# A down projection in Strassen products: its right operands made at the end of the gate and up stage instead of in the projection itself

## The chip, the cores and the metric

The kernel runs on one core of a Trainium2 chip. The metric is the time of one execution on the device, in microseconds (us). Five engines work side by side, each with its own queue of instructions that it takes in order: TensorE (PE, the matmuls), VectorE (DVE), ScalarE (ACT), GpSimd (POOL) and SyncE (SP, which here does nothing but issue DMAs). They wait for one another by semaphores. Matmuls read SBUF and write PSUM banks; a DMA moves between SBUF and DRAM.

## The reference

One layer of a decoder for 1024 tokens of width 1024. Only the last part matters here, the feed-forward network and what follows it:

```python
def _swiglu(h, w_gate, w_up, w_down):
    return (jax.nn.silu(h @ w_gate) * (h @ w_up)) @ w_down
...
        h = _rmsnorm(x, g_ffn[layer]) * (1.0 + sc2) + sh2
        x = x + gt2 * _swiglu(h, w_gate[layer], w_up[layer], w_down[layer])
    return _rmsnorm(x, g_final)
```

The hidden width is 2816, that is 22 blocks of 128. All is float32.

## The kernel before

A float32 product is formed from three matmuls in a shorter format: each operand is split into a high and a low part (`split`: ScalarE casts the high part, another engine, mostly VectorE, subtracts it from the operand to get the low part), and high by high, high by low and low by high are summed in PSUM. On top of this, large products are done by Strassen's scheme in Winograd's form: two by two blocks need 7 products instead of 8, for which sums of blocks are made ahead. Class `Strassen` holds one such group. Its left operands come from weights: `load` fetches a raw tile `Wraw` by SyncE's queue (two buffers), `left` makes the sums `Wsum` on GpSimd (four buffers) and splits each operand into a `Wop` tile (six buffers). `product` runs 3 matmuls for each of the `nk` blocks of the inner dimension, 128x512 each. The right operands, 7 of them in split form, come from a class `Rights`, which makes them of four blocks; they lie in SBUF tiles called `cell`. Results gather in three PSUM banks (a, b, c) of a group; bank a is added to by products 0, 5, 6 and 3 in turn, and what it holds after each is needed, so that it is read between them.

The feed-forward part has three stages.

Gate and up: the 22 blocks of the hidden width are taken two by two. Each of 11 `Pair` objects has one group for gate and one for up, with nk = 4: 14 products of 12 matmuls, 168 in all. `keep` copies bank a to an `x` tile on ScalarE; `g_done` and `u_done` form silu(gate) times up, four tiles of 128x512 for each pair. `st` stores each of these by SyncE to a DRAM tensor `actd`.

Down: the first 20 blocks of the hidden width are taken in 5 chunks of 4. In each chunk there are four groups `Down` with nk = 2 (42 matmuls each), two by two (`dd` = 0 and 1), in which the same right operands are used. 20 groups make 840 matmuls. The right operands of a chunk are made by `dsplit`: it loads the four `actd` blocks back, makes the sums on VectorE (`sub`, line 277), and splits 14 tiles of 128x512 (lines 83 and 84, cell<-cell). This is done one chunk ahead, while the products of `dd` = 1 run. The results are scaled and added to the residual `x1`: of the seven values of a group four are added by VectorE (line 1226) and three are kept by ScalarE (line 1220) and added by GpSimd (line 1228).

Tail: the last two blocks of the hidden width are multiplied without Strassen, and the final norm and the output follow.

The order of the instructions on each engine is set by a scheduler that goes by the order of the code, with a bonus of priority where the code stands under `tc.high_priority`.

## Time and profile before

| | us |
|---|---|
| median of 3 runs | 1693.13 |
| lowest and highest of them | 1692.99, 1709.35 |
| profiled execution | 1701.24 |
| its span, first to last instruction | 1699.5 |
| TensorE busy in the span | 1554.4 (91%) |
| VectorE busy | 1208.4 (71%) |
| ScalarE busy | 864.6 (51%) |
| GpSimd busy | 669.0 (39%) |

The first row is what a changed kernel is compared with. The durations of single instructions come from the profiled execution, whose own time is 8 us above the median. Busy shares are means over stages with different limits, so the stages are read apart: gate and up ends and Down begins near 1420 us after the span's start, the tail begins at 1655 us.

### The profile page before, as it was taken

The page shows a single profiled execution, that of the slowest core. Times are in us where ns is not written, and L with a number is a line of the kernel's source. Part 1 is how long each engine was busy: PE and PEld are TensorE (multiplying, and loading weights), DVE is VectorE, ACT ScalarE, POOL GpSimd, SP SyncE. Part 2 cuts the span into 40 slices and gives each one's busy share as a digit, 9 for nine tenths or more (in the row PEclk, how much of TensorE's full clock was granted, in tenths as well). Part 3 has the DMA queues.
Part 4 walks back from the last instruction along what each step waited for, and adds up shares of the span by engine and source line. Part 5 has one row for each costly group of instructions (what it writes and reads, how often), then busy time and mean ns, then how long its engine had stood idle before and what let it go on. Part 6 is the DMA issues. An engine that isn't in the chain of part 4 may idle for free.

```text
span 1699.5 us, 21993 instructions
## 1 busy us (share of the span) xinstructions
PE 1554.4 (91%) x7306; PEld 1274.6 (75%) x7306; DVE 1208.4 (71%) x2373; ACT 864.6 (51%) x1691; POOL 669.0 (39%) x575
## 2 busy tenths in 40 slices
...
GB/s 328 187 117 306 162 199 241 142 209 207 293 215 179 208 185 214 168 174 138 83 351 143 149 75 93 136 81 100 93 87 93 109 127 241 75 86 88 74 50 99
DMA packets 156065, 267.88 MB, mean 158 GB/s; under 512 B 34844, under 2 KB 70348, under 8 KB 150704
## 3 DMA queue, kind: packets, MB, share of 16 engines
q1 hardware_dynamic: 107952, 224.45, 39.7%
...
## 4 chain that ended last, share of the span: by engine, by line
PE 46%; DVE 11%; DMA 3%; issue 2%; ACT 2%; POOL 1%; DVEq 0%; ACTq 0%; POOLq 0%; SPq 0%
PE bk L219 27%; PE acc L891 3%; PE S L782 3%; DVE Wop L84 3%; PE bk L87 3%; PE bk L88 3%; PE bk L89 3%; DVE cell L84 3%; PE pv L823 2%; PE tr L804 2%; DVE x L1226 2%; DMA vbd<-ev 2%; DVE cell L277 1%; DMA Wraw<-wdown 1%; DVE P L784 0%
## 5 line engine op out<-in xcount | busy, mean ns | idle before, releaser
L219 PE MATMUL bk<-cell,Wop 128*128 128x512 f32 x4056 | 967.3, 399 | 59.3 <-DVE Wop L84 25.2
L219 PEld LDWEIGHTS bk<-cell,Wop 128*128 128x128 f32 x4056 | 769.1, 191 | 251.4 <-DVE Wop L84 40.2
L189 POOL TENSOR_TENSOR Wsum<-Wraw 128x512 f32<-128x512 f32 (+1 forms) x120 | 171.8, 1433 | 533.0 <-DVE Wop L84 310.9
L83 ACT CAST Wop<-Wsum 128x512 fp32r<-128x512 f32 (+1 forms) x241 | 131.5, 548 | 231.2 <-PE bk L219 132.3
L84 DVE TENSOR_TENSOR Wop<-Wsum,Wop 128x512 fp32r<-128x512 f32 (+1 forms) x241 | 182.7, 765 | 90.9 <-ACT Wop L83 89.6
L84 DVE TENSOR_TENSOR Wop<-Wraw,Wop 128x512 fp32r<-128x512 f32 (+2 forms) x182 | 147.6, 818 | 59.6 <-ACT Wop L83 54.4
L83 ACT CAST Wop<-Wraw 128x512 fp32r<-128x512 f32 (+2 forms) x182 | 104.9, 591 | 146.7 <-PE bk L219 60.3
L782 PE MATMUL S<-cell,cell 128*128 128x128 f32 (+8 forms) x480 | 119.1, 363 | 11.8 <-DMA cell<-ksd 7.9
L789 ACT ACTIVATE P<-P,mx 128x512 f32<-128x512 f32 (+7 forms) x128 | 99.3, 778 | 30.7 <-DVE mx L784 18.2
L84 DVE TENSOR_TENSOR pl<-tr,ph 128x512 fp32r<-128x512 f32 (+1 forms) x160 | 98.3, 630 | 22.2 <-ACT ph L83 21.1
L891 PE MATMUL acc<-cell,w 128*128 128x512 f32 x408 | 113.8, 407 | 0.1
L1228 POOL TENSOR_TENSOR x<-x 128x512 f32<-128x512 f32 x60 | 96.2, 1609 | 35.8 <-DVE x L1226 24.8
L162 ACT COPY x<-bk 128x512 f32<-128x512 f32 x92 | 53.4, 586 | 104.2 <-PE bk L219 102.2
L804 PE MATMUL tr<-ident,P 128*128 128x128 f32 x576 | 93.5, 280 | 5.8 <-ACT P L792 4.7
L782 PEld LDWEIGHTS S<-cell,cell 96*128 96x128 f32 (+1 forms) x480 | 80.6, 196 | 21.1 <-DMA cell<-ksd 8.3
L87 PE MATMUL bk<-cell,Wop 128*128 128x512 f32 (+1 forms) x240 | 91.9, 383 | 2.9 <-ACT Wop L83 1.9
L823 PE MATMUL pv<-ph,v 128*128 128x256 f32 (+1 forms) x320 | 88.3, 293 | 6.8 <-ACT ph L83 6.0
L83 ACT CAST ph<-tr 128x512 fp32r<-128x512 f32 (+1 forms) x160 | 83.2, 544 | 15.9 <-PE tr L804 12.7
L88 PE MATMUL bk<-cell,Wop 128*128 128x512 f32 (+1 forms) x240 | 91.0, 380 | 0.0
L89 PE MATMUL bk<-cell,Wop 128*128 128x512 f32 (+1 forms) x240 | 89.8, 377 | 0.0
L891 PEld LDWEIGHTS acc<-cell,w 128*128 128x128 f32 x408 | 77.2, 195 | 13.5 <-DVE ev L922 0.3
L823 PE MATMUL pv<-pl,v 128*128 128x256 f32 x320 | 82.3, 292 | 4.8 <-DVE pl L84 4.5
...
## 6 DMA issues: line engine op xcount, KB each, us to landing
...
```

The costliest lines, as they stand in the source:

```text
L83: ACT.copy(hi, src)
L84: eng.tensor_sub(lo, src, f32(hi))
L87: PE.matmul(ps, w[0], a[0], start=first, stop=False)
L88: PE.matmul(ps, w[0], a[1], start=False, stop=False)
L89: PE.matmul(ps, w[1], a[0], start=False, stop=last)
L189: POOL.tensor_tensor(t, a, b, op=op)
L219: PE.matmul(ps, w[:, wi, k], t[k][:, ti], start=start and k == 0 and n == 0, stop=k == self.nk - 1 and n == 2, skip_group_check=True)
L782: anchor[0] = PE.matmul(s, q[:, i * P:i * P + P], k[:, c * wd:c * wd + wd], start=pi == 0, stop=pi == len(passes) - 1)
L789: ACT.activation(t[:, :n], t[:, :n], AF.Exp, bias=mx[:, 0:1], scale=-1.0, accum_out=mx[:, 1:2])
L804: anchor[0] = PE.transpose(tr[:, co:co + P], self.p[a][:, kb * P:kb * P + P], ident)
L823: anchor[0] = PE.matmul(pv[:, o if l else 0:], v[:, kk], p[:, l:r], start=kk == 0 and n == 0, stop=last and l > 0 and n == 1, skip_group_c ...
L891: PE.matmul(ps, w[wi][:, k0 + k], act(k, ai, hf), start=k == 0 and n == 0, stop=k == nk - 1 and n == 2)
```

## The change

The right operands of Down are no longer made in Down. `u_done` of pairs 0 to 9 splits the operand that a finished tile is by itself (indices 0, 1, 2), and with the pair's last tile makes the four that are sums or differences (four subtractions on VectorE) and splits these. One pair gives one of the two inner blocks of a chunk. Each of the 14 parts is stored by a DMA that ScalarE issues, into the DRAM tensors `tod` (256 KB each). Pairs 0 to 2, whose first tile is made long before the others, store it in `actd` and load it again. Pair 10, which the tail uses, stores as before.

Down then loads the operands in split form, product by product (`load_op`, two loads of 512 KB), one chunk ahead, by SyncE. The products of a group run in another order (`OD`), and all seven values are added to `x1` by VectorE (`into`), with the bonus of priority; nothing is kept by ScalarE or added by GpSimd. The rows of `w_down` are laid out in another order ahead of the launch, to go with the blocks of a pair. A tile `al`, which holds nothing and lies ahead of the cells, grows from 32 to 96 bytes per partition, so that the cells' addresses move by 64 bytes.

```diff
@@ -146,6 +146,7 @@
     actd = [dp.tile([P, T], F32, name=f"actd{f}") for f in range(FFB)]
+    tod = [[dp.tile([P, 2, H], F32, name=f"tod{pr}_{i}") for i in range(7)] for pr in range(FFB // 2 - 1)]
 
@@ -295,7 +296,7 @@
 
-    pool(ctx, "al", side="right").tile([P, 8], F32, name="al")
+    pool(ctx, "al", side="right").tile([P, 24], F32, name="al")
     bq = pool(ctx, "bq", side="right")
@@ -1118,7 +1119,7 @@
         def __init__(self, pr, load=True):
-            self.pr, self.silu = pr, {}
+            self.pr, self.silu, self.early = pr, {}, not load
             self.g = Strassen(wgate[pr], 4, R2.ops, keep, self.g_done, load)
@@ -1138,7 +1139,28 @@
                 DVE.tensor_mul(t, t, s)
-            st(actd[2 * self.pr + pos[0]][:, hsl[pos[1]]], t)
+            f, hf = 2 * self.pr + pos[0], pos[1]
+            if self.pr == FFB // 2 - 1 or pos == (0, 0) and self.early:
+                st(actd[f][:, hsl[hf]], t)
+            elif pos != (0, 1):
+                self.put({(0, 0): 0, (1, 0): 1, (1, 1): 2}[pos], t)
+            else:
+                b0, b1, b2, b3 = [self.silu[p] for p in ((0, 0), (0, 1), (1, 0), (1, 1))]
+                if self.early:
+                    b0 = X()
+                    ld(b0, actd[2 * self.pr][:, hsl[0]])
+                    self.put(0, b0)
+                for o, x_, y in ((b0, b1, b0), (b1, b3, b1), (b3, b3, b0), (b2, b2, b3)):
+                    DVE.tensor_sub(o, x_, y)
+                for i, b in ((5, b3), (4, b0), (6, b1), (3, b2)):
+                    self.put(i, b, True)
+
+        def put(self, i, b, inplace=False):
+            hi = X(F32R)
+            lo = b.bitcast(F32R) if inplace else X(F32R)
+            split(b, hi, lo)
+            for l, t in enumerate((hi, lo)):
+                ACT.dma_start(out=tod[self.pr][i][:, l], in_=f32(t))
 
@@ -1161,6 +1183,7 @@
     p0 = Pair(0)
+    p0.early = True
     p0.steps(OR[:1])
@@ -1188,61 +1211,66 @@
 
-    tcell = cycle([*range(4), *range(8, 26)])
-    rcell = cycle([4, 5, 6, 7, 26, 27])
-    TT = lambda *_: cell(next(tcell))
-
-    def load_act(f):
-        t = cell(next(rcell), dt=F32)
-        t = [t[:, 0], t[:, 1]]
-        ld2(t, actd[f])
-        return t
-
-    def dsplit(f0, nk):
-        R = Rights([load_act(f0 + j) for j in range(2 * nk)], nk, TT, lambda j: DVE)
-        R.early()
-        R.late()
-        return R.ops
-
-    ops = dsplit(0, 2)
-    x1 = [X2() for _ in range(8)]
-    for j in range(8):
-        ld2(x1[j], x1d[j])
+    tcell = cycle(range(28))
+    OD = (0, 1, 5, 4, 6, 2, 3)
+
+    def load_op(ops, ci, i):
+        ops[i] = [cell(next(tcell)) for _ in range(2)]
+        for k in range(2):
+            ld(f32(ops[i][k]), tod[2 * ci + k][i])
+
+    ops = [None] * 7
+    x1 = [None] * 8
+    for n, i in enumerate(OD):
+        load_op(ops, 0, i)
+        if n in (1, 3):
+            for j in ((0, 2), (1, 3))[n // 2]:
+                x1[j] = X2()
+                ld2(x1[j], x1d[j])
 
     class Down(Strassen):
+
+
         def __init__(self, ci, dp_, ops):
             self.dp = dp_
-            super().__init__(wdown[ci * 4 + dp_], 2, ops, self.keep_d, self.done_d)
-
-        def keep_d(self, ps, pos):
-            j = 2 * self.dp + pos[0]
-            t = X()
-            ACT.activation(t, ps, AF.Copy, scale=modc[:, 40 + j:41 + j])
-            return t
-
-        def done_d(self, pos, ps, s):
+            super().__init__(wdown[ci * 4 + dp_], 2, ops, None, None)
+
+        def into(self, name, pos):
             j = 2 * self.dp + pos[0]
             xs = x1[j][pos[1]]
-            DVE.scalar_tensor_tensor(xs, ps, modc[:, 40 + j:41 + j], xs, op0=OP.mult, op1=OP.add)
-            if s is not None:
-                POOL.tensor_add(xs, xs, s)
+            DVE.scalar_tensor_tensor(xs, self.bk[name], modc[:, 40 + j:41 + j], xs, op0=OP.mult, op1=OP.add)
+
+        def step(self, i):
+            name, start, pos = {0: ("a", True, (0, 0)), 1: ("b", True, (0, 0)), 5: ("a", False, (0, 1)),
+                                4: ("c", True, (1, 1)), 6: ("a", False, (1, 1)), 2: ("c", False, (0, 1)),
+                                3: ("a", False, (1, 0))}[i]
+            self.product(i, name, start)
+            with tc.high_priority(offset=HP):
+                self.into(name, pos)
 
...
             prs = [Down(ci, 2 * dd + e, ops) for e in range(2)]
-            if dd == 1:
-                if ci < NC - 1:
-                    nxt = dsplit(4 * ci + 4, 2)
-                else:
-                    tail = []
-                    for f in (20, 21):
-                        raw = load_act(f)
-                        tl = [TT(), TT()]
-                        for hf in range(2):
-                            split(raw[hf], tl[hf][:, 0], tl[hf][:, 1])
-                        tail.append(tl)
-            for i in OR:
+            if ci == 0 and dd == 0:
+                for j in range(4, 8):
+                    x1[j] = X2()
+                    ld2(x1[j], x1d[j])
+            if dd == 0:
+                nxt = [None] * 7
+            if dd == 1 and ci == NC - 1:
+                tail = []
+                for f in (20, 21):
+                    raw = cell(next(tcell), dt=F32)
+                    raw = [raw[:, 0], raw[:, 1]]
+                    ld2(raw, actd[f])
+                    tl = [cell(next(tcell)) for _ in range(2)]
+                    for hf in range(2):
+                        split(raw[hf], tl[hf][:, 0], tl[hf][:, 1])
+                    tail.append(tl)
+            for n, i in enumerate(OD):
+                if ci < NC - 1 and (7 * dd + n) % 2 == 0:
+                    load_op(nxt, ci + 1, OD[(7 * dd + n) // 2])
                 for q in prs:
@@ -1390,7 +1418,8 @@
         "wup": _quarters(g["w_up"][0]),
-        "wdown": np.concatenate([_quarters(g["w_down"][0][i * 512:i * 512 + 512]) for i in range(5)], axis=0),
+        "wdown": np.concatenate([_quarters(g["w_down"][0][i * 512:i * 512 + 512].reshape(2, 2, P, D).transpose(1, 0, 2, 3).reshape(512, D))
+                                 for i in range(5)], axis=0),
         "wdl": _blocks(g["w_down"][0][2560:]).transpose(1, 0, 2).reshape(P, 16, P),
...
```

How the order of instructions moves is shown at three places. First ScalarE between two pairs of gate and up. Before:

```order
L1131 ACTIVATE x<-x 128x512 [waits DVE_49]
L83 CAST Wop<-Wsum 128x512 [waits PE_49,Pool_49]
L162 COPY x<-bk 128x512 [waits PE_49]
L83 CAST Wop<-Wsum 128x512 [waits Activation_49]
L162 COPY x<-bk 128x512 [waits DMAHW6_49,PE_49]
L83 CAST Wop<-Wsum 128x512 [waits Activation_49]
L83 CAST Wop<-Wsum 128x512 [waits PE_49,Pool_49]
```

After, at the same place (COPY is `keep`, `tod` a store, CAST x<-x the split of an operand):

```order
L83 CAST x<-x 128x512 [waits DVE_49]
L83 CAST x<-x 128x512 x2
L83 CAST x<-x 128x512 [waits DVE_49]
L1163 DMA tod_5_200<-x 128x512 [waits DMAHW0_49,Activation_49]
L1163 DMA tod_4_199<-x 128x512 [waits DMAHW2_49,Activation_49]
L1163 DMA tod_5_200<-x 128x512 [waits DMAHW3_49,DVE_49]
L1163 DMA tod_4_199<-x 128x512 [waits DMAHW4_49,DVE_49]
L1163 DMA tod_6_201<-x 128x512 [waits DMAHW5_49,Activation_49]
L1163 DMA tod_6_201<-x 128x512 [waits DMAHW6_49,DVE_49]
L1163 DMA tod_3_198<-x 128x512 [waits DMAHW7_49,Activation_49]
L1163 DMA tod_3_198<-x 128x512 [waits DMAHW0_49,DVE_49]
L163 COPY x<-bk 128x512 x2
```

Behind the last silu product of a pair stand now four casts and eight stores, four of which wait for VectorE; the two copies of the next pair's bank a come after them. Up to the gate and up stage, the rows of all engines are as before, and TensorE's matmuls follow in the same order.

Second, VectorE in a chunk of Down while `dd` = 1 runs. Before:

```order
L1226 SCALAR_TENSOR_TENSOR x<-bk,modc,x 128x512 [waits PE_49]
L84 TENSOR_TENSOR Wop<-Wsum,Wop 128x256 [waits Activation_49]
L84 TENSOR_TENSOR Wop<-Wsum,Wop 128x256 [waits PE_49,Activation_49]
L84 TENSOR_TENSOR cell_13956<-cell_13914,cell_13956 128x512 [waits Activation_49]
L84 TENSOR_TENSOR cell_13957<-cell_13917,cell_13957 128x512 [waits Activation_49]
L1226 SCALAR_TENSOR_TENSOR x<-bk,modc,x 128x512 [waits PE_49]
L84 TENSOR_TENSOR Wop<-Wsum,Wop 128x256 [waits Activation_49] x2
L1226 SCALAR_TENSOR_TENSOR x<-bk,modc,x 128x512 [waits PE_49]
L84 TENSOR_TENSOR cell_13962<-cell_13914,cell_13962 128x512 [waits Activation_49]
L84 TENSOR_TENSOR cell_13963<-cell_13917,cell_13963 128x512 [waits Activation_49]
L84 TENSOR_TENSOR Wop<-Wsum,Wop 128x256 [waits Activation_49]
L1226 SCALAR_TENSOR_TENSOR x<-bk,modc,x 128x512 [waits PE_49]
```

After:

```order
L1241 SCALAR_TENSOR_TENSOR x<-bk,modc,x 128x512 [waits DVE_49,PE_49]
L84 TENSOR_TENSOR Wop<-Wraw,Wop 128x256 [waits DMAHW4_49,Activation_49]
L84 TENSOR_TENSOR Wop<-Wraw,Wop 128x256 [waits Activation_49]
L1241 SCALAR_TENSOR_TENSOR x<-bk,modc,x 128x512 [waits PE_49]
L84 TENSOR_TENSOR Wop<-Wraw,Wop 128x256 [waits Activation_49]
L1241 SCALAR_TENSOR_TENSOR x<-bk,modc,x 128x512 [waits PE_49]
L84 TENSOR_TENSOR Wop<-Wsum,Wop 128x256 [waits Activation_49]
L1241 SCALAR_TENSOR_TENSOR x<-bk,modc,x 128x512 [waits PE_49]
L84 TENSOR_TENSOR Wop<-Wsum,Wop 128x256 [waits Activation_49]
L1241 SCALAR_TENSOR_TENSOR x<-bk,modc,x 128x512 [waits PE_49]
```

The subtractions that make cells are gone, and in their place stand more additions to x1: nearly every split of a `Wop` is now followed by one.

Third, SyncE at the first change of `dd` in Down. Before:

```order
L181 DMA Wraw<-wdown 128x1024 [waits DMAHW7_49,DVE_49,Pool_49]
L181 DMA Wraw<-wdown 128x1024 [waits DMAHW0_49,DVE_49,Pool_49]
L158 DMA cell_13920<-actd_162 128x512 [waits DMAHW1_49,DVE_49]
L158 DMA cell_13920<-actd_162 128x512 [waits DMAHW2_49]
L158 DMA cell_13923<-actd_163 128x512 [waits DMAHW3_49,DVE_49]
L158 DMA cell_13923<-actd_163 128x512 [waits DMAHW4_49]
L181 DMA Wraw<-wdown 128x1024 [waits DMAHW5_49,DMAHW7_49,DVE_49,Pool_49]
L181 DMA Wraw<-wdown 128x1024 [waits DMAHW0_49,DMAHW6_49,DVE_49,Pool_49]
```

After:

```order
L182 DMA Wraw<-wdown 128x1024 [waits DMAHW1_49,DVE_49,Pool_49]
L182 DMA Wraw<-wdown 128x1024 [waits DMAHW2_49,DVE_49,Pool_49]
L1220 DMA cell_14103<-tod_0_202 128x1024 [waits DMAHW3_49,PE_49]
L1220 DMA cell_14104<-tod_0_209 128x1024 [waits DMAHW4_49,PE_49]
L1220 DMA cell_14151<-tod_1_203 128x1024 [waits DMAHW5_49,PE_49]
L1220 DMA cell_14152<-tod_1_210 128x1024 [waits DMAHW6_49,PE_49]
L1220 DMA cell_14205<-tod_5_207 128x1024 [waits DMAHW7_49,PE_49]
L1220 DMA cell_14206<-tod_5_214 128x1024 [waits DMAHW0_49,PE_49]
L1220 DMA cell_14257<-tod_4_206 128x1024 [waits DMAHW1_49,PE_49]
L1220 DMA cell_14258<-tod_4_213 128x1024 [waits DMAHW2_49,PE_49]
L182 DMA Wraw<-wdown 128x1024 [waits DMAHW3_49,DVE_49,Pool_49]
```

Between two fetches of weights (in each case for two groups) stand now eight loads of 512 KB, and in the next gap six, in place of four of 256 KB; they wait for TensorE, which used the cells before, and not for VectorE.

## Rows read from the trace of the kernel before

**Rows 1.** Busy time in 50 us stretches of gate and up; columns in the first line.

```profile
core 0: us, PE busy (x) PEld busy (x) DVE busy (x) ACT busy (x) POOL busy (x), PEclk, DMA share, GB/s
1050.00:1100.00 50.00, 50.00 (x221) 41.04 (x220) 28.72 (x36) 16.14 (x27) 21.84 (x16) 1.00 0.37 132
...
1350.00:1400.00 50.00, 50.00 (x220) 41.07 (x219) 26.43 (x44) 21.55 (x38) 13.13 (x10) 1.00 0.39 132
```

**Rows 2.** The same in 25 us stretches of Down, columns as in rows 1.

```profile
1400.00:1425.00 25.00, 25.00 (x111) 20.49 (x110) 22.70 (x44) 13.04 (x28) 17.86 (x7) 1.00 0.71 230
...
1500.00:1525.00 25.00, 19.92 (x81) 14.28 (x80) 24.97 (x33) 13.03 (x30) 14.87 (x12) 1.00 0.27 84
...
1600.00:1625.00 25.00, 23.97 (x103) 18.86 (x102) 23.66 (x35) 13.97 (x32) 18.39 (x16) 1.00 0.12 43
1625.00:1650.00 25.00, 25.00 (x111) 20.53 (x110) 21.09 (x31) 12.16 (x29) 20.40 (x20) 1.00 0.25 78
```

**Rows 3.** Groups by line and form, 1420 to 1656 us (Down).

```profile
L219 PE MATMUL bk<-cell,Wop 128*128 128x512 f32 x828 | 205.7, 405 | 29.8 <-DVE Wop L84 21.0 <-ACT Wop L83 5.8 <-ACT cell L83 1.5
...
L1228 POOL TENSOR_TENSOR x<-x 128x512 f32<-128x512 f32 x60 | 96.2, 1609 | 35.8 <-DVE x L1226 24.8 <-ACT x L1220 8.3 <-DMA x<-x1d 1.6
L1226 DVE SCALAR_TENSOR_TENSOR x<-bk,modc,x 128x512 f32<-128x512 f32 x78 | 57.3, 739 | 3.5 <-PE bk L219 3.1 <-DMA x<-x1d 0.3
L84 DVE TENSOR_TENSOR cell<-cell,cell 128x512 fp32r<-128x512 f32 x56 | 54.0, 982 | 3.4 <-ACT cell L83 3.4
L84 DVE TENSOR_TENSOR Wop<-Wsum,Wop 128x256 fp32r<-128x256 f32 x79 | 52.4, 677 | 1.0 <-ACT Wop L83 1.0
L1220 ACT ACTIVATE x<-bk,modc 128x512 f32<-128x512 f32 x60 | 41.0, 685 | 15.1 <-PE bk L219 14.9
L84 DVE TENSOR_TENSOR Wop<-Wraw,Wop 128x256 fp32r<-128x256 f32 x56 | 39.7, 727 | 4.7 <-ACT Wop L83 4.7
...
L277 DVE TENSOR_TENSOR cell<-cell 128x512 f32<-128x512 f32 x16 | 15.8, 986 | 0.1
L277 DVE TENSOR_TENSOR cell<-cell,cell 128x512 f32<-128x512 f32 x16 | 15.5, 976 | 0.0
```

**Rows 4.** What TensorE waited for, 1420 to 1656 us: total, times, longest.

```profile
PE bk L219 <- DVE Wop L84: 21.0, 23, 2.8
```

**Rows 5.** The last chunk of Down, columns as in rows 1.

```profile
1614.00:1655.00 41.00, 39.97 (x174) 32.19 (x173) 34.61 (x49) 19.28 (x42) 32.57 (x30) 1.00 0.16 52
```

**Rows 6.** Stretches of 5 us in the last chunk, columns as in rows 1.

```profile
1610.00:1615.00 5.00, 5.00 (x23) 4.12 (x23) 3.93 (x7) 2.91 (x7) 3.32 (x3) 1.00 0.45 170
...
1630.00:1635.00 5.00, 5.00 (x24) 4.09 (x23) 2.12 (x5) 2.62 (x7) 3.20 (x5) 1.00 0.50 184
```

**Rows 7.** VectorE in order of time, in the last chunk: start, us.

```profile
1627.02 0.96 DVE L84 TENSOR_TENSOR Wop<-Wraw,Wop 128x256 fp32r<-128x256 f32 x1
...
1630.88 0.41 DVE L84 TENSOR_TENSOR Wop<-Wsum,Wop 128x256 fp32r<-128x256 f32 x1
```

**Rows 8.** Groups by line and form, 1050 to 1400 us (gate and up).

```profile
L84 DVE TENSOR_TENSOR Wop<-Wsum,Wop 128x512 fp32r<-128x512 f32 x75 | 64.4, 859 | 48.4 <-ACT Wop L83 48.0
...
L83 ACT CAST Wop<-Wsum 128x512 fp32r<-128x512 f32 x75 | 46.6, 622 | 78.9 <-PE bk L219 69.2 <-POOL Wsum L189 9.6
...
L162 ACT COPY x<-bk 128x512 f32<-128x512 f32 x50 | 29.3, 586 | 77.1 <-PE bk L219 77.1
...
L1139 DVE TENSOR_TENSOR x<-bk,x 128x512 f32<-128x512 f32 x28 | 19.3, 690 | 25.1 <-PE bk L219 16.3 <-ACT x L162 8.8
```

**Rows 9.** SyncE in order of time, end of gate and up: start, us.

```profile
1423.12 0.32 SPq L1141 DMA_DIRECT2D actd<-x  x1
```

**Rows 10.** The page: DMA bandwidth by slice, and the queue of SyncE's DMAs.

```profile
GB/s 328 187 117 306 162 199 241 142 209 207 293 215 179 208 185 214 168 174 138 83 351 143 149 75 93 136 81 100 93 87 93 109 127 241 75 86 88 74 50 99
...
q1 hardware_dynamic: 107952, 224.45, 39.7%
```

## The prediction

> **What bounds the kernel now.** I read the busy time by stretches first, because the change touches only the feed-forward part. In gate and up TensorE is busy for the whole of each of the seven stretches of 50 us from 1050 to 1400, of which the first and the last are shown, at a granted clock of 1.00 (the higher of its two levels, 2.4 GHz); VectorE has some 22 to 29 us of work in 50 there, ScalarE 16 to 22 [rows 1]. One matmul of 128x512 costs 50.00 / 220 = 0.2273 us there, and a pair of 168 takes 38.2 us. Nothing can make this stage shorter while the matmuls stay, and they stay.
>
> Down is different. In the seven stretches from 1425 to 1600, of which the one at 1500 is shown, TensorE is busy for some 20 to 22 us in 25, and VectorE for 21 to 25; in the last two stretches, where no operands for another chunk are being made, TensorE is at 23.97 and 25.00 again [rows 2]. The waits agree: of 29.8 us that TensorE stands idle from 1420 to 1656, 21.0 end with VectorE's split of a weight tile [rows 3, 4]. So VectorE bounds Down in four chunks of five. What can be won there: the stretch holds 205.7 + 29.8 = 235.5 us of busy and idle TensorE [rows 3], and 20 groups of 42 make 840 matmuls (828 have records), which at 0.2273 us are 190.9 us. The difference, **44.6 us**, is idle time and the longer matmuls about the gaps. No more than that can come back.
>
> **VectorE in Down, removed and added.** Per chunk it now has 16 additions to x1 at 0.74 us = 11.8, 28 splits of weights at about 0.70 (0.677 and 0.727) = 19.6, and for the operands 14 subtractions at 0.98 = 13.7 and 8 at 0.98 = 7.8 [rows 3]: together 52.9 us against 28 products of 6 matmuls, 28 x 1.364 = 38.2 us. Records of neighbours overlap by some 0.07 us, so that the real load is about 50. After the change the 21.5 us for operands are gone, and 12 more additions to x1 (7 in a group instead of 4) come, 8.9 us: 52.9 - 21.5 + 8.9 = 40.3 us, were the rest as slow as before. It isn't. A split of a weight takes 0.96 us beside a busy GpSimd, and 0.41 us a moment later without it [rows 7]. GpSimd loses its 12 additions of 1.609 us per chunk [rows 3], 19.3 us of the 32.6 that it is busy in the last chunk [rows 5]; 16 sums for weights are left. In the last chunk, which had 16 additions, 28 splits and 4 subtractions for the tail, VectorE was busy 34.6 us beside 32.6 us of GpSimd [rows 5]; with the short durations this would be 16 x 0.67 + 28 x 0.34 + 4 x 0.6, about 22.6 us (starts lie 0.07 closer than durations), so 12.0 us were lost beside GpSimd, 0.37 us for each of its busy microseconds. With 12 to 16 us of GpSimd left, the estimate is 28 x 0.67 + 28 x 0.34 + 0.37 x 14 = 33.5 us, between 28.3 (no loss) and 42.3 (each microsecond of GpSimd is one lost). The middle value rests on the row that is nearest to the new state, the last chunk. **TensorE becomes the bound of Down.** The Trainium skill, SBUF — State Buffer, section Who interferes with whom, says that a VectorE instruction with two inputs in SBUF and a GpSimd instruction that reads SBUF lock each other out, while one with a single SBUF input, as an addition from a PSUM bank has, isn't touched; by it the additions to x1 stay at their 0.74 us, and only the splits can lose, at worst up to the 42.3. The trace agrees that the splits are what varies [rows 7], and its 0.37 says that most of GpSimd's time meets no split.
>
> What stays lost in Down: in the last chunk TensorE was idle for about 1.0 us of 41 [rows 5], though both its refills of weights fell there, at 1610 and 1630, with TensorE at 5.00 of 5 [rows 6]. I take 1 to 2 us for each chunk, 7 in all. At the start of Down the operands of the first chunk are loaded while the last pair runs, but the x1 tiles are queued on SyncE behind stores of this pair: 0 to 4 us, I take 1.
>
> ScalarE in Down loses 14 casts and 12 copies of a bank (0.685 us each) per chunk [rows 3]; it was at half load [rows 2], so this is worth nothing by itself. That a bank is read by VectorE instead costs nothing as long as it is read within the three products (4.1 us) that lie between two products in the same bank; the bonus of priority sees to that.
>
> **Gate and up, added.** Per pair: on ScalarE seven casts at 0.622 = 4.4 us [rows 8], and 14 issues of DMAs; no row has ScalarE issue one, the nearest is SyncE's 0.32 us [rows 9], so 4.5 us, with 0 and three times that as bounds. That raises ScalarE from about 14 to some 23 us in 38.2. On VectorE 11 subtractions at 0.69 to 0.86 [rows 8], 7.6 to 9.5 us, on top of about 19. Neither gets full, and TensorE's work per pair stays 38.2 us. What counts is the order: ScalarE takes its queue in turn, and the last eight stores of a pair stand ahead of the copies of the next pair's bank a. Let T be the end of the old pair's matmuls. The block of casts and stores can start at about T + 5.5, since the cast ahead of it needs a `Wop` tile of the new pair's second product. Four casts, 2.5 us, and eight issues, 2.6 us, end at about T + 11, and VectorE's last split, behind four others of up to 0.86, no later than that. The two copies (0.586 us each [rows 8]) end at T + 12; product 5 of the new pair, which writes bank a again, is after six products of 2.73 us, at T + 16.4. So there are about 4 us of slack, and the next casts of weights have more. I take 0 to 4 us per pair as the bounds and 2 us in all ten pairs together as the value, nearest to the full stretches of rows 1. The stores take 3.7 MB per pair while the DMA engines are busy for 0.37 to 0.39 of the time or less [rows 1]. The Trainium skill, DMA: Bandwidth & Descriptors, section Issuing engines are not separate DMA queues, says that issuing from a second engine saves only the sequencer's issue time; SyncE has that to spare here, so by it the choice of ScalarE buys nothing, and its price is the 4.5 us per pair on ScalarE that the sum has.
>
> The stages ahead of gate and up keep their order; the cells' addresses move by 64 bytes. I put that at 0.
>
> **The sum.** 44.6 - 7 - 1 - 2 = 34.6 us, say 34. The profiled execution, 1701.24 us, would become 1667. It lies 8 us above the median, 1693.13, so the forecast for the median is **1659 us**.
>
> **Rivals.** (1) *Loads bound Down.* Each chunk that loads for the next moves 14 x 0.524 MB of operands and 4 x 0.524 MB of weights, 9.4 MB in 38.2 us, or 247 GB/s, where Down has about 84 now [rows 2]. For it: the fullest stretch near there moved 230 GB/s [rows 2], at which a chunk takes 41 us, and the refills of weights stand behind eight operand loads on SyncE's queue. Against it: the highest slice of the run is 351 GB/s, and SyncE's DMAs moved 224.45 MB in 39.7% of 1699.5 us of the engines, 333 GB/s while at work [rows 10]. At 230 four chunks lose 2.8 us each, and late weights after each refill perhaps 1 us more; the gain falls to about 18, 1675. At 190 GB/s it would be gone. (2) *VectorE stays the bound*: 40.3 us per chunk instead of 38.2 costs 5 x 2.1 = 10.5 us, 1670. With 42.3 it would be 5 x 4.1 = 20.5 us, 1680. (3) *The stores hold up ScalarE*, and the time gets longer: a store that waits for VectorE's low part, or for an earlier DMA, keeps the copies and the casts of weights behind it. From T + 15.2 on for the end of the block each microsecond is one of TensorE's, in each of ten pairs; at T + 19.5, nearly twice the block's length of 5.5, that is 4.3 x 10 = 43 us, more than Down gives back: 1702. Against it: over half of ScalarE's time is free [rows 1]. (4) *The cells' addresses matter* to the matmuls or the DMAs of the attention stages: no row speaks for it, and none shows cells at another address, so I can only bound it by a hundredth of the some 1000 us ahead of gate and up, 10 us either way, 1649 or 1669.
>
> **How the numbers follow.** The forecast has a chance of 0.60, rival 1 0.14, rival 2 0.10, rival 3 0.10, rival 4 0.06. One per cent, 17 us, is about what a measurement tells from no change. Faster by more than that, under 1676: 0.60, 0.08 of rival 1, 0.08 of 2 and 0.05 of 4, or 0.81. Slower, over 1710: 0.04 of rival 3. The rest, 0.15, within 1%. The range goes from 1649, where all of the 44.6 us come back, to 1687, between rivals 1 and 2 at their worse values and rival 3.
>
> **What would show it.** Right: in Down TensorE at 25 us in 25 for most stretches, VectorE under 23, the splits of weights near 0.5 us, GpSimd at a third; gate and up still at 50.00 in 50. Wrong: gaps in gate and up about 16 us after a pair's start that end with ScalarE's copy (rival 3); waits in Down that end with a DMA into `cell` or `Wraw` (1) or with VectorE's split or its addition to x1 (2); changed times ahead of 1000 us (4). The forecast would also be wrong where Down's gaps come from something that VectorE only happened to hide.

## The result, and the profile after

| | before | after |
|---|---|---|
| median, us | 1694.72 (4 runs) | 1677.15 (4 runs) |
| lowest and highest | 1692.99, 1709.35 | 1672.93, 1686.43 |
| profiled execution | 1701.24 | 1676.03 |
| its span | 1699.5 | 1674.2 |

The ratio is 0.9884, with a 95% interval from 0.9847 to 0.9922: 13 to 26 us faster, some 18 to 20 us where 34 were forecast. The profiled spans differ by more, 25.3 us, since the execution profiled of before was 6.5 us above its median and the one of after 1.1 us below.

To see where the time went I cut both traces at the starts of the activation with which ScalarE takes silu from a bank (line 1128, after 1129; one such activation in each of pairs 0, 1 and 3 to 10), at the first addition to x1, and at the first matmul of the tail. All in us:

| stretch | before | after | change |
|---|---|---|---|
| start of the span to pair 0's silu | 1046.4 | 1043.6 | -2.8 |
| pair 0's silu to pair 3's | 93.4 | 103.0 | +9.6 |
| pair 3's to pair 10's | 269.9 | 267.4 | -2.5 |
| pair 10's to the first addition to x1 | 13.6 | 18.8 | +5.2 |
| first addition to the tail's first matmul | 231.9 | 196.3 | -35.6 |
| the tail | 44.4 | 45.0 | +0.6 |

These points lie on ScalarE and VectorE, and the change moves them against TensorE's work: the first addition stands behind the second product of Down before, behind the first after, and in the change it waits for x1 while 36 of Down's 840 matmuls run ahead of it (28 before); pair 0's silu starts 3.9 us later, measured from TensorE's matmuls, than before. The expectations below count by these points. The bottleneck itself is read by counting TensorE's matmuls of the Strassen products. Each trace has all 4056 of them; the last 840 are Down's, and the mark of a pair is set 36 matmuls before its end, where its silu starts when ScalarE is in time. Full pace is the count times the steady time from one matmul's start to the next, 0.2289 us before and 0.2267 after (e1 and e2 tell why):

| stretch, by count of matmuls | before | at its full pace | after | at its full pace | change |
|---|---|---|---|---|---|
| pair 0's mark to pair 3's, 408 | 93.4 | 93.4 | 104.6 | 92.5 | +11.2 |
| pair 3's to pair 10's, 1176 | 269.2 | 269.2 | 269.7 | 266.6 | +0.5 |
| pair 10's to Down's first matmul, 36 | 8.2 | 8.2 | 8.2 | 8.2 | 0.0 |
| first chunk of Down, 168 | 48.1 | 38.5 | 49.7 | 38.1 | +1.6 |
| other four chunks, to the tail's first matmul, 672 | 190.0 | 153.8 | 157.5 | 152.3 | -32.5 |

So the four chunks of Down behind the first gave 32.5 us, the first chunk gave nothing, and 11.7 us were lost in gate and up. With the tail's 0.6 us the kernel is 18.6 us shorter from pair 0's mark on, as the medians have it. The other 6.7 us of the 25.3 lie ahead of this mark (1046.2 us before, 1039.5 after) and can't be told from scatter: in the profiled executions of the kernels below the mark lies between 1036.7 and 1049.6 us.

Busy time by stretches of the kernel after, with the columns of rows 1: two of gate and up, three of Down, three of 5 us about the passage between them, and Down from the first addition to x1 on.

```profile
1050.00:1100.00 50.00, 41.88 (x171) 33.52 (x169) 32.05 (x46) 19.57 (x35) 15.91 (x12) 0.93 0.63 228
...
1150.00:1200.00 50.00, 50.00 (x222) 41.42 (x221) 40.93 (x56) 23.29 (x41) 15.84 (x10) 1.00 0.41 151
...
1475.00:1500.00 25.00, 25.00 (x112) 20.71 (x111) 21.82 (x41) 7.30 (x19) 9.10 (x12) 1.00 0.51 183
1500.00:1525.00 25.00, 24.70 (x109) 19.88 (x108) 20.32 (x36) 6.42 (x17) 6.06 (x8) 1.00 0.76 279
...
1575.00:1600.00 25.00, 25.00 (x112) 20.44 (x110) 21.67 (x41) 9.22 (x23) 8.28 (x11) 1.00 0.19 65
...
1395.00:1400.00 5.00, 2.21 (x10) 1.50 (x8) 1.40 (x4) 0.56 (x2) 0.00 (x0) 1.00 1.05 414
...
1430.00:1435.00 5.00, 1.68 (x5) 1.16 (x4) 4.03 (x9) 0.40 (x1) 0.00 (x0) 0.81 1.05 400
...
1445.00:1450.00 5.00, 1.12 (x5) 0.58 (x4) 1.30 (x2) 0.16 (x1) 0.12 (x1) 1.00 0.88 345
...
1432.80:1629.10 196.30, 187.30 (x804) 152.24 (x804) 158.00 (x274) 52.91 (x134) 54.89 (x72) 0.98 0.54 200
```

In the middle of gate and up TensorE is full, and in Down it works 24.1 to 25 of 25 us in the stretches from 1475 to 1625, of which three are shown (where [rows 2] go down to 19.92), with VectorE at 18.6 to 22.3. But from 1050 to 1100, in pairs 1 and 2, TensorE works only 41.88 of 50 us, and at 1395, 1430 and 1445 it stands. At 1395 and 1430 the DMA share is at 1.0, with 400 GB/s and above.

Groups of instructions of the kernel after in Down (1433 to 1629 us), to set against [rows 3]:

```profile
L220 PE MATMUL bk<-cell,Wop 128*128 128x512 f32 x804 | 187.3, 395 | 9.8 <-ACT Wop L83 6.4 <-DVE x L1241 3.3
...
L1241 DVE SCALAR_TENSOR_TENSOR x<-bk,modc,x 128x512 f32<-128x512 f32 x140 | 103.5, 744 | 20.1 <-PE bk L220 18.8 <-DMA x<-x1d 0.6
L84 DVE TENSOR_TENSOR Wop<-Wsum,Wop 128x256 fp32r<-128x256 f32 x72 | 32.4, 458 | 0.0
L84 DVE TENSOR_TENSOR Wop<-Wraw,Wop 128x256 fp32r<-128x256 f32 x56 | 31.7, 582 | 15.5 <-ACT Wop L83 15.5
...
L190 POOL TENSOR_TENSOR Wsum<-Wraw 128x256 f32<-128x256 f32 x36 | 26.6, 738 | 125.6 <-DMA Wraw<-wdown 91.8 <-DVE Wop L84 33.7
```

The 140 additions to x1 take 0.744 us in the mean, as before (0.739); the splits of weights fell from 677 and 727 ns to 458 and 582, since GpSimd has little left to do. TensorE's idle time is 9.8 us in place of 29.8, and most of it ends with ScalarE's cast of a fresh weight, none with VectorE's split. TensorE in order of time, at the stands of over 2 us behind pair 0's mark (start and length of what follows a stand; the stand and what ended it in brackets):

```profile
1061.55 28.84 PE L220 MATMUL bk<-cell,Wop 128*128 128x512 f32 x120 [2.85 <-ACT x L163]
1095.65 4.36 PE L220 MATMUL bk<-cell,Wop 128*128 128x512 f32 x12 [5.27 <-DVE x L233]
...
1400.07 30.21 PE L220 MATMUL bk<-cell,Wop 128*128 128x512 f32 x132 [2.86 <-ACT x L163]
1433.61 12.51 PE L220 MATMUL bk<-cell,Wop 128*128 128x512 f32 x48 [3.32 <-DVE x L1241]
1450.30 9.99 PE L220 MATMUL bk<-cell,Wop 128*128 128x512 f32 x36 [4.18 <-ACT Wop L83]
```

Line 163 is the copy of bank a, which stands on ScalarE behind the stores of pair 0 and of pair 9; line 233 adds the base, a result of the early pass of pair 2 that is stored and loaded again, and its load came late; line 1241 is the addition to x1, which waited for x1; line 83 is the cast of a weight tile whose refill came late. After four of the five stands, all but the one that ends at 1400, the granted clock is at 0.50 (the lower of its two levels, 1.2 GHz) for 3.4 us, so that a stand costs more than its own length: the two in Down last 7.5 us, and the first chunk is 11.6 us over its full pace.

The chain of waits of the kernel after, at pair 1's last stores and about the end of the last pair (start, length):

```profile
1089.65 8.13 DMA tod<-x
...
1414.73 10.38 DMA actd<-x
...
1425.13 7.65 DMA x<-x1d
...
1441.50 8.24 DMA Wraw<-wdown
```

The chain goes through DMAs: a store of operands, `actd`, `x1`, then the refill of weights. ScalarE in order of time at the same two places (`ACTq` is its queue issuing; what ended the idle time stands in brackets):

```profile
1089.04 8.64 ACTq L1163 DMA_DIRECT2D tod<-x  x6
1097.78 1.14 ACT L83 CAST Wop<-Wsum 128x512 fp32r<-128x512 f32 x2 [8.47 <-DMA tod<-x]
...
1389.02 10.38 ACTq L1163 DMA_DIRECT2D tod<-x  x6
1399.44 1.08 ACT L163 COPY x<-bk 128x512 f32<-128x512 f32 x2 [10.36 <-DMA tod<-x]
```

ScalarE issues six stores in 8.64 us and another six in 10.38 us, where one takes 0.33 us by itself; in between it waits for earlier DMAs to land, and the casts and copies behind it wait with it. By the rows above only the second of these two stands holds TensorE (1400.07); at the first one TensorE waits for the base, and the copy for which it waited before, at 1061.55, stood behind the stores of pair 0.

The DMAs of the kernel after from 1380 to 1440 us (rate by slice of 1.5 us; count, size, median time to landing):

```profile
GB/s 348 1 0 93 322 336 254 317 313 407 408 412 421 410 421 412 421 423 415 421 412 421 412 415 404 412 410 411 396 419 418 408 388 407 404 391 403 400 393 388
...
cell<-tod SPq DMA_DIRECT2D x27, 512.0 KB, 7.7
x<-x1d SPq DMA_DIRECT2D x15, 256.0 KB, 5.3
tod<-x ACTq DMA_DIRECT2D x9, 256.0 KB, 8.3
```

And of before for the same 60 us:

```profile
GB/s 15 0 102 83 0 34 280 305 307 351 284 12 221 134 0 120 229 0 280 173 273 232 231 369 258 362 313 264 315 408 403 406 403 388 385 397 414 213 3 0
...
cell<-actd SPq DMA_DIRECT2D x20, 256.0 KB, 4.5
```

Before moves 300 to 400 GB/s in pieces too, but is at 385 to 414 for only 12 us, from 1423 on, with 20 loads of `actd` of 256 KB; after is at 388 to 423 from 1393 to the end of the window. 27 of the operand loads fall here, where one chunk has 14: the second chunk's loads were let go as well, most of them ahead of x1 and all of them ahead of the refill of weights at 1441. A store of 256 KB takes 8.3 us to land here, where the `actd` stores of before take 2.0 in the median of its page; over all 140 stores of operands the median is 2.9.

### The profile page after: what moved, and what is told of

Its sections match the earlier page's. It is cut to its first block, busy times and chain, and to the rows that moved or that the text cites. A ratio compares the mean times of both kernels' runs of the same rounds, so it can differ in the third digit from the quotient of the medians.

```text
span 1674.2 us, 22241 instructions
## 1 busy us (share of the span) xinstructions
PE 1537.7 (92%) x7306; PEld 1278.2 (76%) x7306; DVE 1240.5 (74%) x2433; ACT 829.8 (50%) x1631; POOL 561.5 (34%) x515
## 3 DMA queue, kind: packets, MB, share of 16 engines
q0 software_dynamic: 48000, 42.04, 11.7%
## 4 chain that ended last, share of the span: by engine, by line
PE 43%; DVE 8%; DMA 8%; ACT 3%; issue 2%; POOL 1%; ACTq 0%; SPq 0%; DVEq 0%; POOLq 0%
PE bk L220 25%; PE acc L892 3%; PE S L783 3%; PE bk L87 3%; PE bk L88 3%; PE bk L89 3%; PE pv L824 2%; DMA Wraw<-wdown 2%; DVE Wop L84 2%; PE tr L805 2%; DMA vbd<-ev 2%; DMA tod<-x 1%; DVE x L1241 1%; DVE cell L84 1%; DMA actd<-x 1%
## 5 line engine op out<-in xcount | busy, mean ns | idle before, releaser
L220 PE MATMUL bk<-cell,Wop 128*128 128x512 f32 x4056 | 951.5, 396 | 51.5 <-DVE x L233 11.0
L190 POOL TENSOR_TENSOR Wsum<-Wraw 128x512 f32<-128x512 f32 (+1 forms) x120 | 156.4, 1304 | 599.0 <-DVE Wop L84 272.2
L84 DVE TENSOR_TENSOR Wop<-Wsum,Wop 128x512 fp32r<-128x512 f32 (+1 forms) x241 | 155.3, 653 | 61.1 <-ACT Wop L83 60.6
L84 DVE TENSOR_TENSOR Wop<-Wraw,Wop 128x512 fp32r<-128x512 f32 (+2 forms) x182 | 152.3, 843 | 39.5 <-ACT Wop L83 35.8
L1241 DVE SCALAR_TENSOR_TENSOR x<-bk,modc,x 128x512 f32<-128x512 f32 x140 | 103.5, 744 | 20.1 <-PE bk L220 18.8
L190 POOL TENSOR_TENSOR Wsum<-Wraw,Wsum 128x512 f32<-128x512 f32 (+1 forms) x60 | 78.5, 1313 | 68.9 <-DVE Wop L84 66.1
L163 ACT COPY x<-bk 128x512 f32<-128x512 f32 x92 | 52.7, 588 | 91.0 <-PE bk L220 48.1
L783 PEld LDWEIGHTS S<-cell,cell 96*128 96x128 f32 (+1 forms) x480 | 80.8, 196 | 18.6 <-DMA cell<-ksd 5.9
```

The lines of the kernel that those rows point to most:

```text
L84: eng.tensor_sub(lo, src, f32(hi))
L190: POOL.tensor_tensor(t, a, b, op=op)
L220: PE.matmul(ps, w[:, wi, k], t[k][:, ti], start=start and k == 0 and n == 0, stop=k == self.nk - 1 and n == 2, skip_group_check=True)
L783: anchor[0] = PE.matmul(s, q[:, i * P:i * P + P], k[:, c * wd:c * wd + wd], start=pi == 0, stop=pi == len(passes) - 1)
L1241: DVE.scalar_tensor_tensor(xs, self.bk[name], modc[:, 40 + j:41 + j], xs, op0=OP.mult, op1=OP.add)
```

## The experiments

Theory A, from these traces and the first table: the change frees Down as forecast, and part of this is lost where DMAs meet, in pairs 1 and 2 (about 9 us) and at the passage into Down (some 5 to 10 us), partly by way of ScalarE, which stands at its stores. The rivals: the addresses of the cells matter (B); the gain comes from the additions on VectorE (C), or is held back by them (D). What the expectations call pair 2's and pair 9's silu is the row of pair 3 and of pair 10 in the first table above; the numbers are the same. Each ratio is to the kernel before, run on the same chip, and since the runs are spread over several chips the ratios are to be compared, not the medians. The stretches are from one profiled execution: two by TensorE's count, two by the marks of the expectations (pair 10's silu to the first addition, and from there to the tail), and Down by count again.

| run | median | ratio, 95% interval | pairs 0 to 3, 408 matmuls | pairs 3 to 10, 1176 | p10 to first addition | from there to the tail | first chunk, 168 | other four, 672 |
|---|---|---|---|---|---|---|---|---|
| before | 1694.72 | 1 | 93.4 | 269.2 | 13.6 | 231.9 | 48.1 | 190.0 |
| the change | 1677.15 | 0.9884 (0.9847 to 0.9922) | 104.6 | 269.7 | 18.8 | 196.3 | 49.7 | 157.5 |
| e1 al 32 bytes | 1677.27 | 0.9887 (0.9843 to 0.9931) | 101.8 | 274.1 | 18.8 | 193.5 | 46.8 | 157.4 |
| e2 before, al 96 bytes | 1690.66 | 0.9974 (0.9951 to 0.9998) | 92.5 | 266.6 | 13.9 | 230.9 | 48.3 | 189.5 |
| e3 old additions | 1674.53 | 0.9867 (0.9822 to 0.9912) | 108.6 | 269.8 | 18.9 | 192.7 | 49.8 | 153.9 |
| e4 x1 first | 1672.76 | 0.9863 (0.9817 to 0.9909) | 107.4 | 271.5 | 11.3 | 202.6 | 49.5 | 156.4 |
| e5 stores by SyncE | 1681.43 | 0.9893 (0.9858 to 0.9927) | 108.4 | 266.6 | 22.3 | 196.6 | 54.1 | 156.8 |
| e6 second chunk late | 1677.83 | 0.9880 (0.9855 to 0.9905) | 106.5 | 271.3 | 11.3 | 202.0 | 47.6 | 157.6 |
| e7 stores spread | 1672.50 | 0.9852 (0.9823 to 0.9882) | 104.8 | 266.8 | 22.5 | 195.4 | 53.5 | 156.5 |
| e8 early pairs later | 1702.46 | 1.0024 (1.0000 to 1.0048) | 92.5 | 305.5 | 19.2 | 196.3 | 50.6 | 157.0 |
| e9 before, new additions | 1685.41 | 0.9909 (0.9880 to 0.9939) | 93.4 | 269.2 | 11.9 | 218.2 | 49.6 | 174.1 |
| e10 refills by ScalarE | 1680.89 | 0.9892 (0.9869 to 0.9916) | 105.1 | 271.5 | 11.3 | 205.7 | 49.9 | 159.1 |
| e11 three together | 1680.24 | 0.9892 (0.9865 to 0.9920) | 105.9 | 267.6 | 11.3 | 206.5 | 50.8 | 159.1 |
| e12 first chunk as before | 1664.62 | 0.9798 (0.9769 to 0.9827) | 92.5 | 269.6 | 11.6 | 203.7 | 51.5 | 156.6 |

By time alone only e2 and e8, slower, and e12, faster, stand apart from the change; the ratios of the others, e9 among them, lie within its interval, and what they tell, they tell by their stretches.

### Addresses: e1 and e2

```diff
-    pool(ctx, "al", side="right").tile([P, 24], F32, name="al")
+    pool(ctx, "al", side="right").tile([P, 8], F32, name="al")
```

> The changed kernel with the tile al at its old 32 bytes, so that the cells lie where they lay before. Theory A (Down gave back about 35 us as forecast, some 8 us were lost again in pairs 1 and 2, where ScalarE stands at its stores, and some 10 us where the last pair passes into Down, where 28 operand loads, the x1 tiles and the weights share the DMA engines): the address does nothing, 1677 us, within 4. Rival B (the address speeds the matmuls up: a pair took 38.45 us before and about 38.1 after, 0.2252 us a matmul in place of 0.2273): slower by 3 us in gate and up alone and by 9 us over all 4056 products' matmuls, 1680 to 1686, with a pair at 38.45 again.

e2 has the reverse edit in the kernel before.

> The kernel before with al at 96 bytes and nothing else. Theory A: 1694 us, within 4, a pair at 38.45 us. Rival B: 1685 to 1691, a pair at about 38.1 us.

The same stretch of e1, and then of e2, busy time with the columns of rows 1:

```profile
1200.00:1250.00 50.00, 50.00 (x220) 41.01 (x220) 39.60 (x53) 24.15 (x43) 15.59 (x10) 1.00 0.48 168
```

```profile
1200.00:1250.00 50.00, 50.00 (x222) 41.42 (x221) 24.50 (x36) 18.57 (x32) 14.66 (x12) 1.00 0.23 84
```

220 matmuls lie in 50 us with the old address, in both kernels, and 222 with the new one, in both kernels. The counts take in matmuls that the ends of the window cut; from start to start, in the mean from 1150 to 1350 us, it is 0.2289 us with the old address (before, e1) and 0.2267 with the new one (after, e2). So rival B is right about the mechanism and a pair is 0.4 us shorter. Over the whole kernel e2 is 0.26% faster, 4 us, the interval just clear of 1; e1 can't be told from the change, where 3 to 9 us were at stake. By e2 the address is some 4 of the 18 to 20 us; e1 can neither confirm nor deny it.

### Which half of the change frees Down: e3 and e9

e3 keeps the operands in DRAM and takes the old additions back:

```diff
-    OD = (0, 1, 5, 4, 6, 2, 3)
+    OD = OR
...
-            super().__init__(wdown[ci * 4 + dp_], 2, ops, None, None)
+            super().__init__(wdown[ci * 4 + dp_], 2, ops, self.keep_d, self.done_d)
...
```

> The changed kernel with the results of Down added as before: four of seven by VectorE, three copied by ScalarE and added by GpSimd, in the old order of products; the operands come from DRAM as in the change. Theory A (what bounded Down was the making of operands on VectorE): VectorE has 16 x 0.74 + 28 x 0.7 = 31 us per chunk, TensorE stays the bound, 1677 us, within 5. Rival C (the seven additions on VectorE are what the gain comes from, since GpSimd's additions slow VectorE down): slower by 10 us or more, TensorE idle behind VectorE in Down. Rival D (the seven additions take VectorE's time and hold Down back): faster by 5 us or more.

e9 makes the operands in Down and has the new additions:

```diff
-            super().__init__(wdown[ci * 4 + dp_], 2, ops, self.keep_d, self.done_d)
+            super().__init__(wdown[ci * 4 + dp_], 2, ops, None, None)
...
+            self.product(i, name, start)
+            with tc.high_priority(offset=HP):
+                self.into(name, pos)
...
-            for i in OR:
+            for i in (0, 1, 5, 4, 6, 2, 3):
```

> The kernel before with Down's seven additions to x1 all on VectorE and the new order of products, while the right operands are still made in Down. Theory A (the operands bound Down): VectorE loses GpSimd's 12 additions as a neighbour and has 12 more of its own; 22 subtractions at 0.61 to 0.68, 28 additions at 0.67, 28 splits at 0.34 and 0.37 x 14 us lost beside GpSimd are about 47 us per chunk against 38.2, where it had about 50; Down at 220 to 235 us, 1685 to 1700. Rival C (the additions are the gain): Down at 200, 1665.

Groups of e3 in Down (1438 to 1631 us):

```profile
L220 PE MATMUL bk<-cell,Wop 128*128 128x512 f32 x803 | 188.0, 396 | 7.2 <-ACT Wop L83 4.8 <-ACT x L1241 2.3
...
L1249 POOL TENSOR_TENSOR x<-x 128x512 f32<-128x512 f32 x59 | 82.1, 1402 | 14.4 <-DVE x L1247 5.6 <-DMA x<-x1d 5.0 <-ACT x L1241 3.6
...
L84 DVE TENSOR_TENSOR Wop<-Wraw,Wop 128x256 fp32r<-128x256 f32 x54 | 43.6, 821 | 29.9 <-ACT Wop L83 29.7
```

Groups of e9 in Down (1425 to 1644 us):

```profile
L219 PE MATMUL bk<-cell,Wop 128*128 128x512 f32 x821 | 199.1, 400 | 18.9 <-ACT Wop L83 6.6 <-DVE Wop L84 6.5 <-DVE x L1220 5.2
...
L1220 DVE SCALAR_TENSOR_TENSOR x<-bk,modc,x 128x512 f32<-128x512 f32 x140 | 102.0, 739 | 6.0 <-PE bk L219 5.8
...
L84 DVE TENSOR_TENSOR cell<-cell,cell 128x512 fp32r<-128x512 f32 x56 | 39.4, 722 | 1.4 <-ACT cell L83 1.4
...
L84 DVE TENSOR_TENSOR Wop<-Wsum,Wop 128x256 fp32r<-128x256 f32 x79 | 33.3, 434 | 0.0
...
L84 DVE TENSOR_TENSOR Wop<-Wraw,Wop 128x256 fp32r<-128x256 f32 x56 | 27.4, 509 | 2.6 <-ACT Wop L83 2.6
```

With the operands moved and the old additions, the four chunks behind the first take 153.9 us, near their full pace of 152.3, though GpSimd's 60 additions (59 have records) slow the splits down to 821 ns: VectorE has room for that. Rival C falls: the gain of Down doesn't need the new additions. Rival D is not settled. By these four chunks the new additions cost 3.6 us (157.5 in place of 153.9, 1.8 of them where the tail's first matmul waits for the last addition), and the times, 0.9867 and 0.9884, can't tell 5 us. Alone the new additions are worth something: e9's four chunks take 174.1 us in place of 190.0, the stretch from the first addition on 218.2 (near theory A's 220 and far from rival C's 200), and the kernel is 0.9% faster than before. Without GpSimd's additions the splits of weights take 434 and 509 ns in place of 677 and 727, and those of operands 722 in place of 982 [rows 3]; with the subtractions, VectorE's groups sum to 225.8 us in place of 234.7, though it has 60 additions of 0.739 us more. The two halves don't add up: each unloads the same engine. By time the change can't even be told from e9; that it is the operands that bound Down rests on the stretches.

### Which engine issues, and in which order: e5, e7, e8

e5:

```diff
-                ACT.dma_start(out=tod[self.pr][i][:, l], in_=f32(t))
+                SP.dma_start(out=tod[self.pr][i][:, l], in_=f32(t))
```

> The changed kernel with all 140 stores of operands issued by SyncE. Theory A1 (ScalarE standing at its stores, 8.5 us in pair 2 and 10.4 us behind pair 9, is what makes TensorE wait there): both stands go, TensorE's two waits for ScalarE's copies with them, 5 to 6 us faster, 1671. Rival A2 (the DMA engines are too full at these places, whoever issues): the waits come back as late weights and late base tiles behind stores on SyncE's queue, 1677 or up to 10 us slower.

e5's waits of TensorE from 1020 to 1150 us, and of SyncE's queue from 1040 to 1110 us:

```profile
PE bk L220 <- DVE x L233: 14.1, 1, 14.1
```

```profile
SPq L1163 <- ACT x L83: 30.7, 9, 9.3
```

ScalarE's stands are gone and so are TensorE's waits for its copies: pairs 3 to 10 run at full pace, 266.6 us. In their place SyncE waits 30.7 us for casts, the bases come behind the stores, and TensorE waits 14.1 us for them at once; at Down's start it waits 6.8 us for x1. Rival A2 is right for the whole: the time is the same. The stores need a queue in which nothing urgent stands behind them, and neither queue is one; GpSimd's was not tried.

e7 (the stores of a pair's last four operands are kept in a list, and set behind a cast of the next pair):

```diff
+                if inplace:
+                    late.append((tod[self.pr][i][:, l], f32(t)))
...
+                if i in (4, 6, 3, 2) and late:
+                    with tc.issue_after(self.u.cast.ins):
+                        for _ in range(2):
+                            o, t = late.pop(0)
+                            ACT.dma_start(out=o, in_=t)
```

> The changed kernel with a pair's last eight stores set two by two behind ScalarE's casts of weights of the next pair, so that its copies of bank a and most casts come first. Theory A1: the 2.9 us wait behind pair 9 goes, and little in pairs 1 and 2, whose casts run on ahead and whose stores stay bunched; 3 to 5 us faster, 1672 to 1674. Rival A2 (full DMA engines): 1677.

Pairs 3 to 10, in which the wait behind pair 9 lies, take 266.8 us in place of 269.7, that is full pace, and pairs 1 and 2 are as in the change, as theory A1 had it. In the same execution the first chunk of Down took 3.8 us longer, so that only the ratio, 0.9852 in place of 0.9884, speaks for a gain, and the intervals overlap.

e8 (pairs 0 to 2 store their tiles; `half` loads them back and splits them, half a pair in each of pairs 3 to 8):

```diff
-            if self.pr == FFB // 2 - 1 or pos == (0, 0) and self.early:
+            if self.pr == FFB // 2 - 1 or self.early:
...
+        def half(self, part):
...
+            if 3 <= pr <= 8:
+                (p0, p1, p2)[(pr - 3) // 2].half((pr - 3) % 2)
```

> The changed kernel with the operands of pairs 0 to 2 made later: these pairs store their four tiles as before, and during pairs 3 to 8 the tiles are loaded back and split, half a pair at a time. Theory A (pairs 0 to 2 lose 9.6 us because the stores of operands meet the loads of weights, of cnd and of the kept bases): from pair 0's silu to pair 2's 93 us as before in place of 103; the added work, 5 subtractions and 4 casts more per pair, stays beside TensorE; 8 to 10 us faster, 1667 to 1669. Rival (the added work fills VectorE, which is at 41 us in 50 there, to 47): pairs 3 to 8 get longer by 1 us each, 1673; where the early loss has another cause, 1677 to 1683.

e8's waits of TensorE from 1140 to 1442 us:

```profile
PE bk L220 <- ACT x L163: 29.1, 10, 6.9
```

The early stretch is at 92.5 us by count, full pace (92.8 by the silu marks): what is lost there in the change comes from the operands of pairs 0 to 2, which are made and stored there. The same work costs only 3.1 us in the seven pairs behind, so that it is not the work alone, but what it meets. For the DMAs, which theory A named, speak the stands in the change that end at 1061.55 and 1095.65, the one behind stores, the other behind a late load. But the work only moved, and cost three times as much where it went: pairs 3 to 10 take 305.5 us in place of 269.7. All the stands end with the copies of bank a behind the stores on ScalarE, 29.1 us in all and up to 6.9 at a time; none ends with VectorE, whose load the rival had named. In the change the pairs in the middle have just enough slack for eight stores behind a pair; with six or eight more in each, and three or four loads, they don't.

### The passage into Down: e4, e6, e10, e11

e4:

```diff
...
                 if ci < NC - 1 and (7 * dd + n) % 2 == 0:
-                    load_op(nxt, ci + 1, OD[(7 * dd + n) // 2])
+                    with (tc.issue_after(last_x1.ins) if ci == 0 else ExitStack()):
+                        load_op(nxt, ci + 1, OD[(7 * dd + n) // 2])
```

> The changed kernel with the second chunk's operand loads kept behind the x1 loads on SyncE. Theory A: the 3.3 us wait for x1 at Down's start goes, and part of ScalarE's 10 us at the stores of pair 9, since 7 MB less are moved there; 5 to 8 us faster, 1669 to 1672. If the first refill of weights still comes late behind the same loads, only 3 us. Rival (the time is lost elsewhere, these waits would be filled by others): 1677.

The first addition comes at 11.3 us as hoped, and Down takes 202.6 us from there: what was won for x1 came back at the refill of weights, for which TensorE waits 7.7 us at once. The first chunk takes 49.5 us, as in the change (49.7).

e6 puts the second chunk's loads behind that refill:

```diff
...
-                if ci < NC - 1 and (7 * dd + n) % 2 == 0:
+                if ci == 0 and dd == 1:
+                    with tc.issue_after(prs[1].raw_ins.ins):
+                        load_op(nxt, 1, i)
+                if 0 < ci < NC - 1 and (7 * dd + n) % 2 == 0:
```

> The changed kernel with the second chunk's operand loads kept behind the first refill of weights of Down on SyncE, so that x1 and this refill come ahead of them. Theory A (28 operand loads ahead of x1 and of the refill cost some 10 us at Down's start): first addition to x1 at 11 us behind pair 9's silu in place of 18.8, Down itself at 196 us or less and not at 202 as with x1 alone put ahead; 8 to 10 us faster than the change, 1667 to 1669. Rival (the second chunk's operands come late then): as x1 first, 1673, or slower.

e6 in stretches of 5 us (columns of rows 1), and SyncE's queue in order of time:

```profile
1445.00:1450.00 5.00, 5.00 (x24) 4.14 (x23) 4.81 (x11) 2.27 (x7) 2.26 (x4) 1.00 1.03 409
...
1465.00:1470.00 5.00, 0.52 (x3) 0.10 (x1) 0.75 (x1) 0.00 (x0) 0.00 (x0) 0.88 1.02 408
1470.00:1475.00 5.00, 0.10 (x1) 0.10 (x1) 0.12 (x1) 0.40 (x1) 0.52 (x1) 0.50 1.02 408
```

```profile
1438.23 1.61 SPq L182 DMA_DIRECT2D Wraw<-wdown  x2
1439.89 23.31 SPq L1220 DMA_DIRECT2D cell<-tod  x22
1464.18 1.60 SPq L182 DMA_DIRECT2D Wraw<-wdown  x2
```

The first refill is in time, TensorE is full at 1445; but now 22 operand loads go out in one piece, the next refill is issued only at 1464.18, behind them, and TensorE stands for 9.4 us. The wait moved by one refill, out of the first 168 matmuls in part (47.6 us), and Down as a whole is 1.9 us shorter than in the change.

e10 takes the refills off that queue (with x1 first, as in e4):

```diff
...
-            ld(self.raw, self.src.rearrange("p (q r) -> p q r", q=4))
+            (ACT.dma_start if nk == 2 else ld)(self.raw, self.src.rearrange("p (q r) -> p q r", q=4))
```

> The changed kernel with x1 loaded ahead of the second chunk's operands, and the refills of weights in Down issued by ScalarE, so that they don't stand behind operand loads on SyncE's queue. Theory A3 (what comes late in Down are the refills, since SyncE's queue holds 8 to 22 operand loads ahead of them, at some 410 GB/s of a full DMA): Down at 190 to 196 us with the first addition 11 us behind pair 9's silu, in place of 202 with x1 alone put ahead; 8 to 10 us faster than the change, 1667 to 1669. Rival (the DMA engines are full whoever asks, and share themselves between the queues): the refills still land 5 us or more late, 1672 to 1677.

e10 in stretches of 10 us (columns of rows 1), and ScalarE in order of time:

```profile
1440.00:1450.00 10.00, 7.58 (x27) 5.48 (x25) 3.81 (x6) 0.40 (x1) 0.00 (x0) 0.84 1.03 410
1450.00:1460.00 10.00, 5.56 (x16) 3.75 (x16) 5.06 (x10) 2.55 (x8) 3.61 (x5) 0.84 1.02 408
```

```profile
1443.03 0.33 ACTq L184 DMA_DIRECT2D Wraw<-wdown  x1
...
1456.08 1.02 ACT L83 CAST Wop<-Wraw 128x256 fp32r<-128x256 f32 x3 [5.09 <-DMA Wraw<-wdown]
```

The rival is right: both refills are issued as soon as their tiles are free, at 1443 and 1449, and the last cast that needs them starts at 1456. A refill takes 7.5 us to land in the median, no less than from SyncE's queue (6.6 in the median of the change's page), and while the two here are under way the engines are at 408 to 410 GB/s. The Trainium skill, DMA: Bandwidth & Descriptors, section Issuing engines are not separate DMA queues, says that DMAs of all issuing engines run on the same 16 DMA engines and interleave there; e5 and e10 agree with it, the one by its time, the other by refills that land no sooner.

e11 joins e10, e7 and an earlier load of the two bases (`ld` of `sps` ahead of pair 1's weights).

> The refills by ScalarE and x1 first as in the run before, the stores set two by two, and the two kept bases of pair 2 loaded ahead of pair 1's weights. Theory A: the waits for the bases in pair 2 (5.3 us) and behind pair 9 (2.9 us) go as well; 12 to 18 us faster than the change, 1659 to 1665. Rival: the waits at pairs 1 and 2 only change places, 1668.

It is no faster than the change. The waits for the bases are gone, and two waits for ScalarE, 4.7 and 4.0 us, stand in their place in pairs 1 and 2; Down has e10's 206 us. In e4, e6, e10 and e11 a wait was moved ahead of another, and none of them is told from the change by its time. None brings the first chunk under 47.6 us, where full pace is 38.1: the trace names x1 and the refills, and what would give these 10 us back is not shown.

### Fewer bytes at both places: e12

e12 also has e4's edit, x1 ahead of the second chunk's loads.

```diff
...
-            if self.pr == FFB // 2 - 1 or pos == (0, 0) and self.early:
+            if self.pr in (0, 1, FFB // 2 - 1) or pos == (0, 0) and self.early:
...
+    R = Rights([load_act(f) for f in (0, 2, 1, 3)], 2, TT, lambda j: DVE)
+    R.early()
+    R.late()
+    ops = R.ops
     x1 = [None] * 8
     for n, i in enumerate(OD):
-        load_op(ops, 0, i)
...
```

> The changed kernel with the first chunk's operands (pairs 0 and 1) made as before, from actd at the end of the last pair, and with x1 loaded ahead of the second chunk's operands; chunks two to five as in the change. 28 stores of pairs 0 and 1 and 7.3 MB of operand loads at the end of gate and up are gone, and 22 subtractions come to VectorE in the last pair, which makes no operands itself. Theory A (the gain that is missing was lost to DMAs that meet: the stores of pairs 0 to 2 with loads, and the operand loads of two chunks with x1 and the refills): from pair 0's silu to pair 2's 93 to 97 us in place of 103, first addition to x1 12 to 14 us behind pair 9's silu, Down at 193 to 198; 12 to 16 us faster than the change, 1661 to 1666. Rival (making operands in the last pair holds TensorE up again, as at the start of Down before): first addition at 18 us or later, 1672 or more.

It is the fastest kernel of the study, 2.0% under before and 0.9% under the change, with intervals that don't touch. TensorE in order of time from 1035 to 1110 us in e12, its waits from 1380 to 1655, and the chain of waits from 1410 to 1450:

```profile
1034.64 75.64 PE L222 MATMUL bk<-cell,Wop 128*128 128x512 f32 x333
```

```profile
PE bk L222 <- ACT Wop L83: 11.7, 4, 9.1
```

```profile
1425.83 5.96 DMA cell<-tod
...
1431.87 10.73 DMA Wraw<-wdown
```

The early stretch is at 94.5 us by the silu marks and at 92.5 by count: TensorE runs through it without a stand, so that all of the 12.1 us that the change loses in pairs 0 to 2 come from making and storing the operands of pairs 0 and 1 there. The first addition comes at 11.6 us, though VectorE makes operands in the last pair; the rival falls. Down is at 203.7 us and not under 198: x1 and eight operand loads still stand ahead of the second refill, which TensorE awaits for 9.1 us. So e12 wins at one of the two places alone. At the passage its fewer bytes gave nothing: the five chunks take 208.1 us by count, in the change 207.2. That the 9 us could be had too was not tried. The ratios of e12 and of the change differ by some 15 us, of which the traces show these 12.1.

## Why the prediction was right, and where it was short

**What bounds Down** was right. VectorE's making of operands was the bound (e3, e9, and the four chunks behind the first), and without it TensorE is. VectorE's load was put at 33.5 us per chunk, between 28.3 and 42.3; from the first addition to the tail it is busy for 158.00 us, or 31.6 per chunk, the tail's few splits included. The middle of the estimate was a little high: it took the loss beside GpSimd to fall in proportion to GpSimd's work. The Trainium skill's rule (SBUF — State Buffer, Who interferes with whom) agrees with both kinds of rows: additions that read one input from SBUF stay at 0.739 to 0.744 us with GpSimd busy or not, splits with two go from 821 ns (e3) to 582 (after).

**What stays lost in Down**, 7 us in five chunks, was of the right size outside the first chunk: 157.5 - 152.3 = 5.2 us in four. The ground on which it stood, 44.6 us, was close too. It came from 0.2273 us a matmul, a count over a window that takes in matmuls cut by its ends; from start to start it is 0.2289, and the 840 matmuls, which took 238.1 us before, had 45.8 us to give at that pace, 47.7 at the pace of the new address.

**The sum** of 34.6 us missed at three terms. The start of Down, put at 1, cost 11.6 in the first chunk. Gate and up, put at 2, lost 12.1 us in pairs 0 to 2 and 3.1 behind pair 9. Against that the address, put at 0, gave 3.5 us in gate and up and 1.9 in Down. So Down gave 30.9 where 44.6 - 7 - 1 = 36.6 were forecast, gate and up got 11.7 longer, the tail 0.6, and 18.6 are left.

**The start of Down** is where a step failed: "the operands of the first chunk are loaded while the last pair runs". It is true, and so are the second chunk's: their cells are free as soon as the last pair has used them, and nothing in the program holds the loads. 28 loads of 512 KB, x1 and the stores then fill the DMA engines for some 50 us. Rival 1 named the mechanism, refills that stand behind operand loads, but worked it out as a steady rate, 247 GB/s against 230 to 351. In the steady state the engines carry it (up to 279 GB/s in 25 us, with TensorE at 24 to 25 us in 25). What costs is the burst at the passage, where the ring of cells is filled twice. How much of the 11.6 us less traffic alone would give back is open: e12, without the first chunk's loads, has them too.

**Rival 3**, ScalarE held up by its stores, had a chance of 0.10. In the change ScalarE's copies held TensorE behind two pairs of ten, 0 and 9, for 2.9 us each; behind pair 1 ScalarE stood for 8.5 us, and TensorE waited for the base. The sum of the slack, 4 us, was right where the DMA engines were at 0.39 to 0.49 of the time, and the pairs in the middle bear it out, 50.00 in 50. It left out that a store's issue waits for earlier DMAs to land, which the text had named among the reasons without giving it a duration: at the two places of the stands landing took some 8 us in place of 2. (The end of the block at T + 19.5, called nearly twice its length, makes it 14 us, over two and a half times the 5.5.) e8 shows the rival in full, with one and a half operand sets in a pair: 35.8 us longer in pairs 3 to 10, and no faster than before.

**Rival 4**, the addresses, was right in kind with a weight of 0.06, and small; it showed in the matmuls of gate and up and of Down. In the stages ahead, where the rival had put it, no run tells it from scatter.

**The range**, 1649 to 1687, held the time because rivals 1 and 3 were in it; the likeliest case alone would have been 18 us off. That is luck in part: what these rivals describe happened at other places and for other lengths than they were priced by.
